# Packed compression, two VectorE jobs moved to ScalarE, and the gates last in the hybrid mixers

## The chip, the core and the metric

The kernel runs on one core of one Trainium2 chip. The metric is the device time of one execution in microseconds (us), lower is better. TensorE multiplies; VectorE (DVE in the profile), ScalarE (ACT) and GpSimd (POOL) do the rest; SyncE (SP) issues most weight loads.

## The reference, cut to what matters

Two blocks of two layers each transform a 256 x 1024 activation in float32. Every layer is a SwiGLU feed-forward, a mixer, and a second feed-forward. The change touches only the mixer of the second block (twice per execution). That mixer projects the normalised activation to many parts and runs three kinds of attention on them: stick-breaking attention (4 heads), NSA attention (8 heads, with a compressed, a selected and a window branch) and DSA attention (4 heads, keys picked by an index). Three gates then weigh their projections:

```python
def nsa_compress(x, pe, w1, w2):      # 256 tokens -> 15 blocks of 32 tokens, stride 16, 2 groups
    blocks = blocks + pe
    flat = blocks.reshape(15, 2, 32 * 64)
    return silu(flat @ w1) @ w2       # w1: 2048 x 128, w2: 128 x 64

kc = rms_norm(nsa_compress(k_cmp, ...)); vc = nsa_compress(v_cmp, ...)
g_a, g_b, g_c = split(sigmoid(h @ w_gate), 3)
merged = g_a * (o_a @ w_br_a) + g_b * (o_b @ w_br_b) + g_c * (o_c @ w_br_c)
return merged @ w_out
```

The compression yields 30 rows (15 blocks, 2 groups) of keys and 30 of values.

## The kernel before, in words

Dense products (`dense`, line 134 to 136 inside `mm3`) split every float32 weight tile into a high and a low part: a ScalarE cast (line 330) and a VectorE subtraction (line 331), two 128 x 512 weight rows at a time, called a pair here. Each pair then takes 12 matmuls (2 weight rows, 2 token tiles, 3 products). Weights arrive as units of 1 MB through SP (line 107) into a pool `raw` of 4 slots. In `mixer2` the split parts live in three slots of high parts and as many of low parts. Dense results accumulate in the PSUM pool `acc` (3 banks), attention in `at` (4 banks).

`mixer2` (from line 684) first defines its pieces and then calls them one by one at the end. Six `chunk_*` calls are dense products that give the queries, keys and values, with norms and rotations on VectorE behind them. `nsa(kz, vo, br, t, p)` is one attention step: two to four matmuls for the scores (line 880), a softmax and the product with the values in `attend` (lines 361 to 394), and the scaled result into `ob` (line 890 for branch 1, line 892 for branch 2, which adds). `attend` transposes the probabilities P by four TensorE instructions (line 385), copies them out of PSUM on VectorE (line 387), and multiplies them with the values (line 392). `dsa` uses it too, and so does the first block's `mixer1`, which passes its mask as a list. There are 15 such steps in a `mixer2`. `index` and `topk` (16 rounds, lines 843 and 844) choose DSA's keys. `stick` is the stick-breaking attention, `cmp` the compressed branch.

`compress` (line 656) runs once for keys and once for values: it transposes a piece of `z`, adds a position term on VectorE (line 665), loads `w1` (1 MB, line 667) into a `raw` slot and runs 16 accumulating float32 matmuls with 30 weight columns and 128 moving columns (line 672). A sigmoid, a product, a transpose of 30 rows (line 677) and one matmul with `w2` (line 681) follow. A float32 matmul is two TensorE instructions, each with its own weight load, so 16 matmuls are 32 instructions.

`gate(c)` is a dense product over 8 weight rows: two loads, four pairs, 48 matmuls, and two ScalarE copies out of PSUM (line 944). There are six. The sigmoid is applied later through tanh (line 1003).

The order in which each engine gets its instructions is not the order of the text: the framework schedules while it simulates a timeline, takes the earlier instruction in program order where several are ready, and so fixes a static order per engine. Moving a call in the text moves its priority. After the last piece the three results are transposed (line 229) and multiplied with `w_br_*`, and the result with `w_out`.

Of the kernel before, what the change touches and what calls it, by code (L numbers as in the profile page):

```python
# [10 lines left out]
F32 = mybir.dt.float32  # L11
F32R = mybir.dt.float32r
I32 = mybir.dt.int32
AF = mybir.ActivationFunctionType
ALU = mybir.AluOpType
# [3 lines left out]
P = 128  # L19
# [7 lines left out]
class Net:  # L27
# [332 lines left out]
    def attend(self, sc, ns, v, mask=None):  # L360
        nc = self.nc
        w = ns * P
        nh = 4 // ns
        nm = self.sm.tile([P, nh], F32, name=self.nm("nmx"), tag=f"nmx{nh}")
        src = sc
        if mask is None:
            nc.vector.tensor_reduce(nm, sc.rearrange("p (h e) -> p h e", h=nh), axis=AX, op=ALU.max, negate=True)
        else:
            src = self.b("ms")
            for j in range(nh):  # L370
                s = slice(j * w, (j + 1) * w)
                m = mask[j] if isinstance(mask, list) else mask
                nc.vector.tensor_tensor_reduce(out=src[:, s], in0=sc[:, s], in1=m, scale=1.0, scalar=-3e38,
                                               op0=ALU.add, op1=ALU.max, accum_out=nm[:, j : j + 1])
            nc.vector.tensor_single_scalar(nm, nm, -1.0, op=ALU.mult)  # L375
        den = self.sm.tile([P, nh], F32, name=self.nm("den"), tag=f"den{nh}")
        pr = self.b("pr")
        for j in range(nh):
            s = slice(j * w, (j + 1) * w)
            nc.scalar.activation(pr[:, s], src[:, s], AF.Exp, bias=nm[:, j : j + 1], accum_out=den[:, j : j + 1])  # L380
        rc = self.sm.tile([P, nh], F32, name=self.nm("rc"), tag=f"rc{nh}")
        nc.vector.reciprocal(rc, den)
        tp = sc
        for q in range(4):
            nc.tensor.transpose(tp[:, q * P : (q + 1) * P], pr[:, q * P : (q + 1) * P], self.ident)  # L385
        pt = self.b("pt")
        nc.vector.tensor_copy(pt, tp)
        po = tp
        for j in range(nh):
            for st in range(ns):  # L390
                q = slice((ns * j + st) * P, (ns * j + st + 1) * P)
                nc.tensor.matmul(po[:, j * 64 : (j + 1) * 64], lhsT=pt[:, q], rhs=v(j, st), start=(st == 0),  # L392
                                 stop=(st == ns - 1))
        return po[:, : nh * 64].rearrange("p (j d) -> p j d", j=nh), rc
# [164 lines left out]
class Mix2:  # L559
    def consts2(self):  # L560
        nc, a = self.nc, self.a
        self.c2r = self.cst2.tile([P, 4, P], F32R, name="c2r")
        st = self.raw.tile([P, 4, 512], F32, name="rawc2", tag="raw").rearrange("p a b -> p (a b)")[:, :512]
        nc.scalar.dma_start(out=st, in_=a["c2m"])
        nc.scalar.copy(self.c2r.rearrange("p a b -> p (a b)"), st)
        self.mcaus, self.mstr, self.ntri, self.none = (self.c2r[:, i] for i in range(4))
        self.idr = self.cst2.tile([P, P], F32R, name="idr")
        nc.scalar.copy(self.idr, self.ident)
        self.mc32 = self.cst2.tile([P, 2 * P], F32, name="mc32")
        nc.gpsimd.memset(self.mc32[:, :P], 0.0)  # L570
        nc.scalar.dma_start(out=self.mc32[:, P:], in_=a["c2m"][:, 0:P])
        self.c2v = self.cst2.tile([P, 288], F32, name="c2v")
        nc.scalar.dma_start(out=self.c2v[:, :286], in_=a["c2v"])
        v = self.c2v
        tt = lambda q: q.rearrange("p (t d) -> p t d", t=2)
        self.rope = (tt(v[:, 0:32]), tt(v[:, 32:48]), tt(v[:, 48:64]))
        self.ropei = (tt(v[:, 64:80]), tt(v[:, 80:88]), tt(v[:, 88:96]))
        self.cmpm = tt(v[:, 96:126])
        self.ropec = (v[0:30, 126:142].unsqueeze(1), v[0:30, 142:150].unsqueeze(1), v[0:30, 150:158].unsqueeze(1))
        self.expand = v[0:30, 158:278]  # L580
        self.bmask = v[0:120, 278:286]
        self.one = self.cst2.tile([P, 32], F32, name="one")[:, :1]
        nc.gpsimd.memset(self.one, 1.0)
        self.pet = self.cst2.tile([P, 2, 2, 16], F32, name="pet")
        nc.scalar.dma_start(out=self.pet, in_=a["pet"])

# [66 lines left out]
        self.nc.scalar.copy(kz[0:64, 0, :], tp[0:64, :256])  # L653
        self.nc.vector.tensor_copy(kz[64:128, 1, :], tp[64:128, :256])

    def compress(self, l, kv, z, hid):
        nc, a = self.nc, self.a
        tp = self.tpair(lambda g, t: z[:, t, (kv * 2 + g) * P : (kv * 2 + g + 1) * P])
        xg = self.b("rl")[:, :480].rearrange("p (k g c) -> p k g c", k=16, g=2)
        for lp in range(2):  # L660
            b = slice(64 * lp, 64 * lp + 64)
            tv = tp[b].rearrange("p (g c k) -> p k g c", g=2, k=16)
            pe = lambda k0: self.pet[b, l, kv, k0 : k0 + 8].unsqueeze(2).unsqueeze(2).broadcast_to([64, 8, 2, 15])
            for hf in range(2):
                nc.vector.tensor_tensor(xg[b, hf * 8 : hf * 8 + 8], tv[:, lp::2, :, hf : hf + 15], pe(hf * 8), op=ALU.add)
        w1 = self.raw.tile([P, 4, 512], F32, name=self.nm("w1"), tag="raw").rearrange("p a (b n) -> p (a b) n", n=P)
        nc.sync.dma_start(out=w1, in_=a["nsa_cmp_w1_2"][l, kv].rearrange("(k p) n -> p k n", p=P))
        w2 = self.b("cw2", 64)
        nc.scalar.dma_start(out=w2, in_=a["nsa_cmp_w2_2"][l, kv])
        ph = self.psum(self.at)  # L670
        for k in range(16):
            nc.tensor.matmul(ph[:30, :P], lhsT=xg[:, k].rearrange("p g c -> p (g c)"), rhs=w1[:, k],  # L672
                             start=(k == 0), stop=(k == 15))
        th = self.b("cth", P, pp=30)
        self.sigm(th, ph[:30, :P])
        nc.vector.tensor_mul(th, th, ph[:30, :P])
        nc.tensor.transpose(ph[:, P : P + 30], th, self.ident[:30, :30])
        hT = self.b("chT", 32)[:, :30]
        nc.vector.tensor_copy(hT, ph[:, P : P + 30])
        po = ph[:30, 256:320]  # L680
        nc.tensor.matmul(po, lhsT=hT, rhs=w2, start=True, stop=True)
        nc.vector.tensor_copy(hid, po)

    def mixer2(self, l, nxt):
        nc, a = self.nc, self.a
# [78 lines left out]
            return z  # L764

        def compress(z):
            self.compress(l, 0, z, hk)
            self.compress(l, 1, z, vc)
            hv = hk.unsqueeze(1).unsqueeze(1)
            self.headnorm(hv, 1, 1, [(0, 1, gn(1))], 0, pp=30)  # L770
            self.do_rope(hv, self.ropec, 8, 1, 1, pp=30)
            dup = self.b("dup", P, 1, pp=30)
            vec.tensor_copy(dup.rearrange("p (a d) -> p a d", a=2), hk.unsqueeze(1).broadcast_to([30, 2, 64]))
            tp = self.psum(self.at)
            nc.tensor.transpose(tp[:, :30], dup, self.ident[:30, :30])
            vec.tensor_copy(kcz[0:64, 0, :], tp[0:64, 0:15])
            vec.tensor_copy(kcz[64:128, 1, :], tp[64:128, 15:30])
            pv = tp
            mm(pv[:120, :64], lhsT=self.expand, rhs=vc, start=True, stop=True)
            vx = self.b("vx", 64, 1, pp=120)  # L780
            vec.tensor_copy(vx, pv[:120, :64])
            vec.tensor_tensor(vbd, vx.unsqueeze(1).broadcast_to([120, 8, 64]),
                              self.bmask.unsqueeze(2).broadcast_to([120, 8, 64]), op=ALU.mult)
# [90 lines left out]
        def nsa(kz, vo, br, t, p):  # L874
# [10 lines left out]
            for i in range(nu):  # L885
                for j in range(2):
                    o = ob[:, t, (4 * j + p + i) * 64 : (4 * j + p + i + 1) * 64]
                    k = 2 * i + j
                    if br == 1:
                        vec.tensor_scalar(out=o, in0=po[:, k], scalar1=rc[:, k : k + 1], scalar2=None, op0=ALU.mult)  # L890
                    else:
                        vec.scalar_tensor_tensor(o, po[:, k], rc[:, k : k + 1], o, op0=ALU.mult, op1=ALU.add)

# [57 lines left out]
        nsa(kzs, 256, 1, 0, 0)  # L951
        nsa(kzs, 256, 1, 1, 1)
        nsa(kzs, 256, 1, 1, 2)
        gate(0)
        chunk_b()
        nsa(kzs, 256, 1, 0, 2)
        chunk_d()
        w0 = index(0)
        nsa(kzs, 256, 1, 1, 3)
        w1 = index(1)  # L960
        nsa(kzw, 384, 2, 0, 2)
        nsa(kzw, 384, 2, 1, 3)
        chunk_f()
# [1 line left out]
        topk(1, w1)  # L965
        stick(0)
        nsa(kzw, 384, 2, 0, 0)
        gate(1)
        compress(zc)
        nsa(kzw, 384, 2, 1, 0)  # L970
        nsa(kzw, 384, 2, 1, 1)
        gate(4)
        stick(1)
        cmp(0)
        nsa(kzw, 384, 2, 1, 2)
        cmp(1)
        gate(2)
        gate(3)
        dsa(0, 0)
        dsa(1, 0)  # L980
        gate(5)
        dsa(1, 1)

        oT = {}
        for nm_, o, kk in (("a", oa, 2), ("b", ob, 4), ("c", oc, 2)):
# [171 lines left out]
```

## Time and profile before

| | us |
|---|---|
| median of 3 runs (2275.8 to 2280.51) | 2279.7 |
| the profiled execution's own time | 2279.99 |
| its span, first to last instruction | 2278.2 |
| TensorE busy in the span | 2255.0 |
| VectorE, ScalarE, GpSimd busy | 1548.1, 1148.5, 78.1 |

Times in the rows are counted from the span's start. TensorE's instructions are pipelined: an instruction's own duration holds the way through the array, and the next one starts before it ends. What an instruction costs TensorE is therefore the distance from its start to the next start. PE is the matmul side, PEld the weight loads beside it; an arrow in brackets names what ended an engine's idle time.

### The profile page before, as it was taken

What the parts mean: (1) busy time and instruction counts of PE and PEld (TensorE: products, weight loads), DVE (VectorE), ACT (ScalarE), POOL (GpSimd) and SP (SyncE); (2) the same over time, 40 slices, a digit from 0 to 9 for tenths busy, and PEclk for the clock granted to TensorE, in tenths of its full rate; (3) what the DMA queues carried; (4) which work ended last, traced back from release to release, by engine and by line L of the source; (5) the groups of instructions that cost most, each with busy time, mean ns of one, the idle gap of its engine ahead of it and who ended that gap; (6) DMA issues with size and microseconds to landing.
All of it is one profiled execution on the core that took longest, in us unless ns stands there. A gap on an engine that the chain in (4) does not pass through costs nothing.

```text
span 2278.2 us, 27621 instructions
## 1 busy us (share of the span) xinstructions
PE 2255.0 (99%) x10446; PEld 1858.3 (82%) x10446; DVE 1548.1 (68%) x2549; ACT 1148.5 (50%) x1674; POOL 78.1 (3%) x133
## 2 busy tenths in 40 slices
PE   9999999999999999999999999999999999999999
PEld 7888888888788888887888887788887888778787
DVE  5667766665666776667576896766656678877564
ACT  5445545454454545445454555554544455465443
POOL 0001000000001000000000000000000000000000
PEclk9999999999999999999999999999999999999999
DMA  7767545766676655676776534467667755425673
GB/s 260 249 237 237 188 166 185 252 238 204 221 259 218 206 176 184 223 263 201 240 244 208 184 111 130 148 212 244 238 202 238 242 183 159 134 89 186 222 252 126
DMA packets 241669, 464.68 MB, mean 204 GB/s; under 512 B 22176, under 2 KB 47392, under 8 KB 239488
## 3 DMA queue, kind: packets, MB, share of 16 engines
q1 hardware_dynamic: 212272, 397.44, 52.6%
q0 software_dynamic: 14320, 60.69, 7.5%
q10 hardware_dynamic: 14944, 4.79, 1.1%
q8 instruction: 82, 1.34, 0.2%
q14 instruction: 51, 0.42, 0.1%
HBM read 433.00 MB, written 29.88 MB: 203 GB/s over the span
## 4 chain that ended last, share of the span: by engine, by line
PE 88%; issue 7%; DMA 3%; DVE 1%; ACT 1%; DVEq 0%; POOLq 0%; ACTq 0%
PE ps L134 27%; PE ps L135 27%; PE ps L136 27%; PE ps L392 2%; DMA hT<-hop 1%; DMA hop<-hB 1%; PE ps L385 1%; PE ps L880 1%; PE ps L672 1%; PE ps L209 1%; DVE wlo L331 0%; PE ps L825 0%; PE ps L229 0%; ACT whi L330 0%; DVE hlo L331 0%
## 5 line engine op out<-in xcount | busy, mean ns | idle before, releaser
L331 DVE TENSOR_TENSOR wlo<-raw,whi 128x1024 fp32r<-128x1024 f32 (+2 forms) x754 | 907.7, 1211 | 533.6 <-ACT whi L330 515.7
L330 ACT CAST whi<-raw 128x1024 fp32r<-128x1024 f32 (+2 forms) x754 | 777.6, 1043 | 772.7 <-PE ps L136 731.8
L135 PE MATMUL ps<-wlo,xhi 128*128 128x512 f32 (+2 forms) x2048 | 798.2, 391 | 4.3 <-DVE wlo L331 4.2
L134 PE MATMUL ps<-whi,xhi 128*128 128x512 f32 (+2 forms) x2048 | 784.4, 392 | 6.3 <-ACT whi L330 6.0
L136 PE MATMUL ps<-whi,xlo 128*128 128x512 f32 (+2 forms) x2048 | 788.2, 389 | 0.0
L135 PEld LDWEIGHTS ps<-wlo,xhi 128*128 128x128 f32 x2048 | 385.7, 188 | 85.7 <-DVE wlo L331 7.8
L134 PEld LDWEIGHTS ps<-whi,xhi 128*128 128x128 f32 x2048 | 384.1, 188 | 87.0 <-ACT whi L330 8.5
L136 PEld LDWEIGHTS ps<-whi,xlo 128*128 128x128 f32 x2048 | 385.4, 188 | 77.5 <-issue 0.5
L135 PE MATMUL ps<-wlo,hhi 128*128 128x512 f32 x704 | 273.9, 389 | 0.0
L136 PE MATMUL ps<-whi,hlo 128*128 128x512 f32 x704 | 273.9, 389 | 0.0
L134 PE MATMUL ps<-whi,hhi 128*128 128x512 f32 x704 | 271.3, 389 | 0.0
L136 PEld LDWEIGHTS ps<-whi,hlo 128*128 128x128 f32 x704 | 132.1, 188 | 27.5
L134 PEld LDWEIGHTS ps<-whi,hhi 128*128 128x128 f32 x704 | 132.2, 188 | 27.4
L135 PEld LDWEIGHTS ps<-wlo,hhi 128*128 128x128 f32 x704 | 132.1, 188 | 27.4
L84 DVE STREAM_TRANSPOSE hB<-h 128x1024 f32<-128x1024 f32 (+2 forms) x72 | 98.9, 1387 | 2.9 <-DMA hop<-hB 2.7
L331 DVE TENSOR_TENSOR hlo<-hT,hhi 128x512 fp32r<-128x512 f32 (+1 forms) x96 | 57.1, 642 | 55.5 <-ACT hhi L330 55.2
L330 ACT CAST hhi<-hT 128x512 fp32r<-128x512 f32 (+1 forms) x96 | 49.8, 582 | 85.2 <-DMA hT<-hop 85.2
L261 ACT ACTIVATE sl<-ps,rstd 128x512 f32<-128x512 f32 (+1 forms) x96 | 62.3, 651 | 50.9 <-PE ps L136 46.8
L86 POOL DMA_DIRECT2D hop<-hB x43 | 23.5, 547 | 1743.3 <-ACT whi L330 858.0
L380 ACT ACTIVATE pr<-ms,nmx 128x256 f32<-128x256 f32 (+1 forms) x112 | 51.3, 461 | 43.3 <-DVE nmx L375 38.6
L263 DVE SCALAR_TENSOR_TENSOR h<-ps,rstd,sl 128x512 f32<-128x512 f32 (+1 forms) x96 | 65.1, 698 | 3.7 <-ACT sl L261 1.9
L87 POOL DMA_DIRECT2D hT<-hop x39 | 29.5, 757 | 187.4 <-DMA hop<-hB 94.1
(352 smaller groups left out, 1708.0 us busy)
## 6 DMA issues: line engine op xcount, KB each, us to landing
raw<-in_ffn_w_gu_dram SPq DMA_DIRECT2D x80, 1024.0 KB, 5.2
raw<-in_ffn_w_in_dram SPq DMA_DIRECT2D x79, 1024.0 KB, 5.2
raw<-in_ffn_w_out_dram SPq DMA_DIRECT2D x40, 1024.0 KB, 5.5
raw<-in_ffn_w_down_dram SPq DMA_DIRECT2D x40, 1024.0 KB, 5.3
raw<-in_mix_w_in_dram SPq DMA_DIRECT2D x32, 1024.0 KB, 6.3
raw<-in_w_gate_dram SPq DMA_DIRECT2D x24, 1024.0 KB, 5.2
hop<-hB POOLq DMA_DIRECT2D x16, 1024.0 KB, 5.8
hT<-hop POOLq DMA_DIRECT2D x16, 1024.0 KB, 6.3
```

The source lines that it names most:

```text
L84: nc.vector.transpose(ov[:, :, :, t, :], src(t)[:, : nk * P].rearrange("p (k i c) -> p k c i", c=4, i=32))
L86: nc.gpsimd.dma_start(out=hop.rearrange("q (i c) n -> (q i) (c n)", c=4), in_=hb)
L87: nc.gpsimd.dma_start(out=tile[:, :n].rearrange("p (q n) -> p q n", q=4), in_=hop.rearrange("q p n -> p q n"))
L134: mm(ps[:, :n], lhsT=lh, rhs=hi, start=start, stop=False)
L135: mm(ps[:, :n], lhsT=lh, rhs=lo, start=False, stop=False)
L136: mm(ps[:, :n], lhsT=ll, rhs=hi, start=False, stop=stop)
L261: nc.scalar.activation(sl[:, :w], gs[t][:, :w], AF.Silu, scale=rs[:, t : t + 1])
L263: nc.vector.scalar_tensor_tensor(h[t][:, o : o + w], us[t][:, :w], rs[:, t : t + 1], sl[:, :w], op0=ALU.mult, op1=ALU.mult)
L330: self.nc.scalar.copy(hi, src)
L331: return self.nc.vector.tensor_sub(lo, src, hi.bitcast(F32))
L380: nc.scalar.activation(pr[:, s], src[:, s], AF.Exp, bias=nm[:, j : j + 1], accum_out=den[:, j : j + 1])
L392: nc.tensor.matmul(po[:, j * 64 : (j + 1) * 64], lhsT=pt[:, q], rhs=v(j, st), start=(st == 0), stop=(st == ns - 1))
```

## The change

The two compressions of a mixer become one call. Both inputs are prepared with 32 columns (two are zeroed by GpSimd), both `w1` are loaded, and the 32 matmuls write to four groups of 32 PSUM partitions, chosen by keys or values and by the parity of k. A product with a constant `fold` matrix adds the two parities; sigmoid, product and transpose then run once for both. The call moves ahead of the window branch. In the second mixers, P is copied out of PSUM by ScalarE, and branch 1's results are scaled by ScalarE. The six gates are called after everything else, in the order 0, 1, 4, 2, 3, 5.

```diff
@@ attend
-        nc.vector.tensor_copy(pt, tp)
+        (nc.vector.tensor_copy if isinstance(mask, list) else nc.scalar.copy)(pt, tp)
@@ consts2
+        self.fold = self.cst2.tile([P, 64], F32, name="fold")
+        nc.vector.tensor_add(self.fold, self.ident[:, :64], self.ident[:, 64:])
@@ compress
-    def compress(self, l, kv, z, hid):
+    def compress(self, l, z, hids):
+        xgs, w1s, w2s = [], [], []
+        for kv in range(2):
...
+            xg = self.b("rl").rearrange("p (k c) -> p k c", k=16)
+            nc.gpsimd.memset(xg[:, :, 30:32], 0.0)
...
+            nc.sync.dma_start(out=w1, in_=a["nsa_cmp_w1_2"][l, kv].rearrange("(k p) n -> p k n", p=P))
...
         ph = self.psum(self.at)
         for k in range(16):
-            nc.tensor.matmul(ph[:30, :P], lhsT=xg[:, k].rearrange("p g c -> p (g c)"), rhs=w1[:, k],
-                             start=(k == 0), stop=(k == 15))
-        th = self.b("cth", P, pp=30)
-        self.sigm(th, ph[:30, :P])
-        nc.vector.tensor_mul(th, th, ph[:30, :P])
-        nc.tensor.transpose(ph[:, P : P + 30], th, self.ident[:30, :30])
...
+            for kv in range(2):
+                r = 32 * (2 * (k % 2) + kv)
+                nc.tensor.matmul(ph[r : r + 32, :P], lhsT=xgs[kv][:, k], rhs=w1s[kv][:, k],
+                                 start=(k < 2), stop=(k > 13))
+        part = self.b("cpp", P, 1)
+        nc.vector.tensor_copy(part, ph[:, :P])
+        hs = ph[:64, P : 2 * P]
+        nc.tensor.matmul(hs, lhsT=self.fold, rhs=part, start=True, stop=True)
+        th = self.b("cth", P, 1, pp=64)
+        self.sigm(th, hs)
+        nc.vector.tensor_mul(th, th, hs)
+        nc.tensor.transpose(ph[:, 256:320], th, self.ident[:64, :64])
+        hT = self.b("chT", 64, 1)
+        nc.vector.tensor_copy(hT, ph[:, 256:320])
+        for kv in range(2):
+            po = ph[:30, 320 + 64 * kv : 384 + 64 * kv]
+            nc.tensor.matmul(po, lhsT=hT[:, 32 * kv : 32 * kv + 30], rhs=w2s[kv], start=True, stop=True)
+            nc.vector.tensor_copy(hids[kv], po)
@@ nsa
                     if br == 1:
-                        vec.tensor_scalar(out=o, in0=po[:, k], scalar1=rc[:, k : k + 1], scalar2=None, op0=ALU.mult)
+                        act.activation(o, po[:, k], AF.Copy, scale=rc[:, k : k + 1])
@@ order of the calls
         nsa(kzs, 256, 1, 1, 2)
-        gate(0)
         chunk_b()
...
         w1 = index(1)
+        compress(zc)
         nsa(kzw, 384, 2, 0, 2)
...
         nsa(kzw, 384, 2, 0, 0)
-        gate(1)
-        compress(zc)
         nsa(kzw, 384, 2, 1, 0)
         nsa(kzw, 384, 2, 1, 1)
-        gate(4)
         stick(1)
         cmp(0)
         nsa(kzw, 384, 2, 1, 2)
         cmp(1)
-        gate(2)
-        gate(3)
         dsa(0, 0)
         dsa(1, 0)
-        gate(5)
         dsa(1, 1)
+        for c in (0, 1, 4, 2, 3, 5):
+            gate(c)
```

## Rows read from the trace of the kernel before

**Rows 1.** The page: the chain that ended last, by engine.
```profile
PE 88%; issue 7%; DMA 3%; DVE 1%; ACT 1%; DVEq 0%; POOLq 0%; ACTq 0%
```
**Rows 2.** Stretches: busy us (instructions) of PE, PEld, DVE, ACT, POOL; PE's granted clock.
```profile
1240.00:1472.00 232.00, 231.19 (x1186) 187.46 (x1185) 188.69 (x539) 129.15 (x247) 2.89 (x7) 1.00 0.44 141
...
1330.00:1350.00 20.00, 20.00 (x91) 14.40 (x89) 19.79 (x78) 12.80 (x30) 0.00 (x0) 1.00 0.33 107
1417.00:1431.50 14.50, 13.96 (x91) 10.32 (x89) 13.26 (x61) 8.29 (x28) 0.00 (x0) 1.00 0.10 36
2023.50:2039.20 15.70, 15.16 (x90) 11.62 (x89) 13.53 (x61) 8.30 (x28) 0.00 (x0) 0.89 0.11 35
2027.40:2030.80 3.40, 3.40 (x15) 2.93 (x14) 2.47 (x15) 0.30 (x1) 0.00 (x0) 0.50 0.15 57
```
**Rows 3.** Line 672 in the first second-block mixer: count, durations (ns), first and last start.
```profile
L672 PEld LDWEIGHTS ps<-w,rl x64: 104/108/108, 1365.0 to 1376.5; 128*30 128x30 f32 x64
L672 PE MATMUL ps<-w,rl x64: 272/273/295, 1365.0 to 1376.6; 128*30 128x128 f32 x64
```
**Rows 4.** Timeline of PE around line 672: start, us, instructions merged (x how many).
```profile
1371.33 1.06 PE L672 MATMUL ps<-w,rl 128*30 128x128 f32 x8
1372.32 1.10 PE L925 MATMUL ps<-va,se 128*128 128x64 f32 x8
1373.36 1.93 PE L672 MATMUL ps<-w,rl 128*30 128x128 f32 x16
1375.22 1.10 PE L392 MATMUL ps<-va,pt 128*128 128x64 f32 x8
```
**Rows 5.** Timeline of PE where lines 681 and 677 run between dense matmuls.
```profile
1381.75 0.40 PE L135 MATMUL ps<-wlo,xhi 128*128 128x512 f32 x1
1381.99 0.40 PE L136 MATMUL ps<-whi,xlo 128*128 128x512 f32 x1
1382.32 0.30 PE L681 MATMUL ps<-cw,chT 128*30 128x64 f32 x2
1382.55 0.74 PE L134 MATMUL ps<-whi,xhi 128*128 128x512 f32 x2
1383.21 0.24 PE L677 MATMUL ps<-ident,cth 30*128 30x30 f32 x1
1383.38 0.50 PE L134 MATMUL ps<-whi,xhi 128*128 128x512 f32 x1
```
**Rows 6.** Groups of the first second-block mixer: busy us, mean ns, idle before and releasers.
```profile
L331 DVE TENSOR_TENSOR wlo<-raw,whi 128x1024 fp32r<-128x1024 f32 x54 | 65.8, 1221 | 14.6 <-ACT whi L330 14.3
L330 ACT CAST whi<-raw 128x1024 fp32r<-128x1024 f32 x53 | 55.5, 1047 | 37.8 <-PE ps L136 36.6 <-ACT whi L330 0.7
...
L387 DVE COPY pt<-ps 128x512 f32<-128x512 f32 x15 | 10.1, 685 | 0.9 <-PE ps L385 0.9
...
L890 DVE TENSOR_SCALAR ob<-ps,rc 128x64 f32<-128x64 f32 x16 | 3.7, 277 | 1.1 <-PE ps L392 1.1
...
L817 ACT COPY oth<-ps 128x512 f32<-128x512 f32 x1 | 0.6, 592 | 0.0
...
L636 ACT ACTIVATE va<-ps,rstd 128x64 f32<-128x64 f32 x1 | 0.3, 315 | 0.0
```
**Rows 7.** SP's loads in the same mixer: start, us from first to last, count.
```profile
1303.82 9.49 SPq L667 DMA_DIRECT2D w<-in_nsa_cmp_w_dram  x2
1320.96 59.98 SPq L107 DMA_DIRECT2D raw<-in_w_gate_dram  x8
```
**Rows 8.** Timeline of PE where float32 transposes fall between dense matmuls.
```profile
1403.51 0.48 PE L135 MATMUL ps<-wlo,xhi 128*128 128x512 f32 x1
1403.83 0.60 PE L385 MATMUL ps<-ident,pr 128*128 128x128 f32 x4
```
**Rows 9.** Groups of topk in the same mixer, shapes merged.
```profile
L843 DVE MAX8 m<-work 128x8 f32<-128x128 f32 (+1 forms) x16 | 5.7, 355 | 0.0
L844 DVE MATCH_REPLACE8 work<-m,work 128x128 f32<-128x128 f32 (+1 forms) x16 | 5.5, 344 | 0.0
```

More of the change, by code (lines that the diff above doesn't have):

```diff
@@ L654, in zevac @@
         self.nc.vector.tensor_copy(kz[64:128, 1, :], tp[64:128, :256])
-    def compress(self, l, kv, z, hid):
+    def compress(self, l, z, hids):
         nc, a = self.nc, self.a
[L658 to L669, printed above, removed]
+        xgs, w1s, w2s = [], [], []
+        for kv in range(2):
+            tp = self.tpair(lambda g, t: z[:, t, (kv * 2 + g) * P : (kv * 2 + g + 1) * P])
+            xg = self.b("rl").rearrange("p (k c) -> p k c", k=16)
+            nc.gpsimd.memset(xg[:, :, 30:32], 0.0)
+            xv = xg[:, :, :30].rearrange("p k (g c) -> p k g c", g=2)
+            for lp in range(2):
+                b = slice(64 * lp, 64 * lp + 64)
+                tv = tp[b].rearrange("p (g c k) -> p k g c", g=2, k=16)
+                pe = lambda k0: self.pet[b, l, kv, k0 : k0 + 8].unsqueeze(2).unsqueeze(2).broadcast_to([64, 8, 2, 15])
+                for hf in range(2):
+                    nc.vector.tensor_tensor(xv[b, hf * 8 : hf * 8 + 8], tv[:, lp::2, :, hf : hf + 15], pe(hf * 8),
+                                            op=ALU.add)
+            w1 = self.raw.tile([P, 4, 512], F32, name=self.nm("w1"), tag="raw").rearrange("p a (b n) -> p (a b) n", n=P)
+            nc.sync.dma_start(out=w1, in_=a["nsa_cmp_w1_2"][l, kv].rearrange("(k p) n -> p k n", p=P))
+            w2 = self.b("cw2", 64)
+            nc.scalar.dma_start(out=w2, in_=a["nsa_cmp_w2_2"][l, kv])
+            xgs.append(xg), w1s.append(w1), w2s.append(w2)
@@ L670, in compress @@
         ph = self.psum(self.at)
         for k in range(16):
-            nc.tensor.matmul(ph[:30, :P], lhsT=xg[:, k].rearrange("p g c -> p (g c)"), rhs=w1[:, k],
-                             start=(k == 0), stop=(k == 15))
-        th = self.b("cth", P, pp=30)
-        self.sigm(th, ph[:30, :P])
-        nc.vector.tensor_mul(th, th, ph[:30, :P])
-        nc.tensor.transpose(ph[:, P : P + 30], th, self.ident[:30, :30])
-        hT = self.b("chT", 32)[:, :30]
-        nc.vector.tensor_copy(hT, ph[:, P : P + 30])
@@ L680, in compress @@
-        po = ph[:30, 256:320]
-        nc.tensor.matmul(po, lhsT=hT, rhs=w2, start=True, stop=True)
-        nc.vector.tensor_copy(hid, po)
+            for kv in range(2):
[6 more added lines that the diff above has]
+        nc.tensor.matmul(hs, lhsT=self.fold, rhs=part, start=True, stop=True)
@@ L766, in compress @@
         def compress(z):
-            self.compress(l, 0, z, hk)
-            self.compress(l, 1, z, vc)
+            self.compress(l, z, (hk, vc))
             hv = hk.unsqueeze(1).unsqueeze(1)
```

## The prediction

> **What bounds the kernel now.** I read the chain that ended last first: it runs through TensorE for 88% of the span [rows 1]. So a microsecond counts only if it comes off TensorE's own stream, or if it opens or closes a gap in that stream. The busy time by stretch shows the second-block mixer, 232 us long, with TensorE busy for 231.19 of them, VectorE for 188.69 and ScalarE for 129.15 [rows 2]; the second layer's mixer repeats it. Even in a stretch where VectorE is busy for 19.79 of 20 us TensorE has no gap [rows 2]. The only gaps stand at the end of the attention, some 0.54 us in each layer (13.96 of 14.50, 15.16 of 15.70) [rows 2]. In the second layer that same end takes 15.70 us instead of 14.50, and 3.4 us of it have a granted clock of 0.50, the 1.2 GHz level, just after a thin stretch of short matmuls [rows 2]. So the argument goes by distances from start to start on TensorE, not by the durations in its rows.
>
> **What the compression costs TensorE now.** Per mixer line 672 issues 64 instructions [rows 3]. A run of 16 of them lasts 1.86 us until the next line starts and a run of 8 lasts 0.99 us [rows 4]; the difference, 0.87 us for 8, gives 0.109 us for each instruction, and 0.12 us remain for leaving the 30-column form. So 64 x 0.109 = 7.0 us. The other forms cannot start under this one: a dense matmul that is followed by line 681 takes 0.33 us to the next start where its neighbour takes 0.24, so entering costs 0.09; the two dense ones after it take 0.66 instead of 0.48, which is one return and the next entry, 0.09 each [rows 5]. Line 681 itself takes 0.23 and line 677 0.17 [rows 5]. In the timeline the 64 instructions, first at 1365.0 and last at 1376.6 [rows 3], come in eight runs with attention matmuls between them: 8 x (0.12 + 0.09) = 1.7 us. The two visits of line 681 cost 0.41 each, those of line 677 0.35 each, together 1.5. Sum: 10.2 us per mixer.
>
> **What it costs after.** There are still 32 float32 matmuls and so 64 instructions, now in four groups of 32 output partitions. The two halves of one matmul go to the same group and must follow each other; the next matmul's first half goes to another group. If groups run side by side, a pair of halves should cost one distance, not two: 32 x 0.109 = 3.5 us. No row of the profile shows two column groups, so I bound it: 7.0 us if nothing overlaps, 1.75 if all four groups do, and above 7.0 if a change of group costs what a change of form costs (below). I take 3.5, since the order of the halves forbids four at a time and since the weights of 30 columns are already hidden now (a load of 108 ns beside a matmul every 109 [rows 3, 4]). To it come: three runs rather than eight, as one accumulation holds both (3 x 0.21 = 0.6; between 1 and 8 runs 0.2 to 1.7); the fold product, two halves and a change of form, 2 x 0.109 + 0.21 = 0.4; one transpose, 0.35; the two products with w2 together, 0.41 + 2 x 0.054 = 0.5. Sum 5.4, so 4.8 us less per mixer and **9.6 us in both**.
>
> **What moves beside it.** P's copy takes 685 ns on VectorE, 15 times; ScalarE's copy of the same shape out of PSUM takes 592 [rows 6]. Branch 1's scaling takes 277 ns, 16 times, against 315 for ScalarE's scaled copy of 128 x 64 [rows 6]. VectorE goes from 189 to 174 us of the 232, ScalarE from 129 to 143. I cost this at nothing, because TensorE covers it; without that cover each attention step would be 0.1 us shorter by the copy and some 0.1 longer by the scalings. Queued behind a copy that waits for its transposes are ScalarE's weight casts, and behind those VectorE's subtractions and TensorE. What hides a late cast are the three pair slots: two further pairs are 24 matmuls, 5.8 us at 0.24 [rows 5], less 1.05 for the cast and 1.22 for the subtraction [rows 6], so a pair may be 3.5 us late. The compression's small VectorE work (one copy and one sigmoid instead of two sigmoids), the zeroing on GpSimd, busy for 2.89 of 232 us [rows 2], and the one-time fold matrix lie under the same cover.
>
> **The gates.** Moved, per mixer, are 6 x 48 = 288 dense matmuls on TensorE, 24 casts on ScalarE and as many subtractions on VectorE, 12 copies out of PSUM on ScalarE, and 12 loads on SP, past all chunks, the attention and both w1 loads; POOL's queue has nothing of them. None is added or dropped. As the lowest in order they fill what attention leaves, up to its very end. That may close the 0.54 us gaps and keep the clock at 2.4 GHz at the second layer's end: 2 x 0.54 + 1.2 = 2.3 us at best [rows 2]. Against it, float32 work between dense matmuls costs an entry each time: a dense matmul before four transposes takes 0.32 instead of 0.24 [rows 5, 8]. The end stretches hold 88 to 91 instructions in some 24 pieces each; dense work between half of them is 2 x 12 x 0.08 = 1.9 us. I put the two together at nothing, with 2 us either way. The w1 loads now claim two of the four raw slots early; they already did, from 1303.82 until line 672 ran at 1365, while gate loads went through the other two without a gap on TensorE [rows 2, 3, 7]. After the change they should be freed sooner, so I cost it at nothing.
>
> **The sum.** The profiled execution took 2279.99 us (span 2278.2 and 1.8 around it); 2279.99 - 9.6 = 2270.4. The median of the runs shown, 2279.7, lies 0.3 below, so I say **2270**.
>
> **Rivals.** **No overlap of groups (0.22).** Each instruction keeps 0.109 us. Then 7.0 + 1.9 = 8.9 instead of 10.2, 2.6 us less in all, 2277.4. This is also the case in which the packing does not do what it says; for it speaks that no row shows overlap between instructions of this form.
> **Four groups at once (0.15).** 1.75 + 1.9 = 3.7, so 6.5 less per mixer: 2267.0. Against it: halves of one group stand next to each other. The Trainium skill (TensorEngine Tiling (Array Packing), Theoretical Speedup) gives up to 4x for 32 columns; by that rule the time is this rival's, and no row here shows it.
> **A change of group drains the array (0.05).** Then every pair costs what leaving costs now, 2 x 0.109 + 0.12 = 0.34, and 32 of them 10.8 us; with the 1.9 that is 2.5 more per mixer, 2285. The start of a load beside each running matmul [rows 3, 4] speaks against it, but all these loads go to one group. The Trainium skill (TensorE: Matmul & The Clock Gate, Part 3, The mechanism) says that weight loads slip under a running matmul only where the row group differs. All four column groups use the same 128 rows, so by it the change would go this rival's way; rows 3 and 4 disagree, as load and matmul of the same rows fit in one distance.
> **The gates starve (0.14), slower.** Their casts and subtractions are last in order on both engines. If VectorE runs topk's dependent rounds, 5.7 + 5.5 = 11.2 us per mixer [rows 9], in one block ahead of a waiting subtraction, the 3.5 us of cover run out and TensorE stands for 7.7 us: per mixer 2.9 more than now, 2285.8. It decides from 4.8 us of gap per mixer on. For it: gate 0 stood ahead of topk in order, and VectorE is busy for 19.79 of 20 us there [rows 2]. Against it: the change takes 14 us off VectorE, and chunks go first.
>
> **How the numbers follow.** The forecast has 0.44. A measurement of this kernel tells about 0.2% from no change, 4.6 us. Forecast and four groups are faster: 0.59. No overlap is within: 0.22. Drain and starving are slower: 0.19. The range reaches from four groups with the better clock (2267.0 - 2.3, about 2264) to no overlap with the bad end, many runs and a part of a starved gate (2282); it leaves out the 0.19 that are slower.
>
> **What would show it.** Right: line 672's successor still 64 instructions per mixer, with pairs 0.11 us apart, few runs, TensorE busy throughout, the last dense matmuls of a gate after the last attention matmul, and no 0.50 clock at the second mixer's end. Wrong: distances of 0.109 throughout (no overlap), 0.03 (four groups) or 0.17 on average (drain); gaps on TensorE ended by lines 330 or 331 (starving), or ScalarE casts that wait behind P's copy.

## The result, and the profile after

The changed kernel is slower: 2311.27 us median of 6 runs (2303.52 to 2316.35) against 2280.11 of 6 before (2275.8 to 2282.56), ratio 1.0136 [1.0117, 1.0155]. The forecast was 2270 with a range to 2282. The profiled execution took 2310.99, 31.0 more than the one of before.

Lines of after differ by some ten to fifteen: the compression's matmuls are line 682, its fold product 687, its transpose 691, the product with `w2` 696, the transpose of `dup` (the compressed keys written twice, for the score product) 789, an NSA step's scores 894, stick's scores 913, a gate's copy out of PSUM 958, tanh 1013; 920 to 922 are stick's functions on ScalarE, 874 the exponential of `cmp`. Four lines of the page (span, PE's busy time, the PE clock in 40 slices, the chain that ended last):

```profile
span 2309.2 us, 27640 instructions
...
PE 2268.2 (98%) x10448; PEld 1864.8 (81%) x10448; DVE 1527.7 (66%) x2482; ACT 1180.6 (51%) x1742; POOL 78.8 (3%) x137
...
PEclk9999999999999999999999997999999999989999
...
PE 83%; issue 7%; DMA 4%; DVE 3%; ACT 2%; DVEq 0%; ACTq 0%; POOLq 0%
```

TensorE's share of the chain fell from 88% [rows 1] to 83%, and two slices have a lower clock, one in each second-block mixer. The view of stretches gives the place (PE, PEld, DVE, ACT, POOL busy; PE's granted clock):

```profile
1392.00:1460.00 68.00, 58.03 (x269) 45.06 (x268) 35.68 (x122) 41.43 (x85) 0.00 (x0) 0.81 0.20 62
2015.00:2082.00 67.00, 57.26 (x270) 44.66 (x269) 36.02 (x122) 41.81 (x85) 0.00 (x0) 0.82 0.19 63
1400.00:1420.00 20.00, 15.65 (x74) 11.86 (x74) 10.23 (x45) 14.16 (x32) 0.00 (x0) 0.74 0.09 29
1420.00:1440.00 20.00, 17.02 (x58) 12.16 (x56) 9.71 (x46) 7.24 (x21) 0.00 (x0) 0.66 0.00 1
```

The ends of the attention, 0.54 us of idle TensorE each before [rows 2], now hold 9.97 and 9.74 us of it, and the mean clock there is 0.81 and 0.82, a mix of the 2.4 and the 1.2 GHz level. At those clocks 68 and 67 us lose 0.19 x 68 + 0.18 x 67 = 25.0 us' worth of work, against 1.7 before (3.40 us at 0.50 [rows 2]). By this estimate the ends cost 18.6 + 23.3 us; less the 13.0 that the packing should bring with four groups side by side, that is 28.9 of the 31.0. It is no more than an estimate, since some of the low clock falls on idle time and so is counted twice. It puts the loss at the two ends, gap and clock at about the same weight; the lengths of the two mixers, read below, are 30.4 us more together.

Why the ends are bare shows in TensorE's timeline of the first such mixer (start, us, instructions merged; the dense ones left out):

```profile
1342.03 1.00 PE L392 MATMUL ps<-va,pt 128*128 128x64 f32 x8
1342.96 0.41 PE L682 MATMUL ps<-w,rl 128*32 128x128 f32 x2
...
1350.74 1.95 PE L682 MATMUL ps<-w,rl 128*32 128x128 f32 x62
...
1357.81 0.43 PE L687 MATMUL ps<-cpp,fold 128*64 128x128 f32 x2
...
1365.74 0.27 PE L691 MATMUL ps<-ident,cth 64*128 64x64 f32 x1
1370.26 0.30 PE L696 MATMUL ps<-cw,chT 128*30 128x64 f32 x2
1374.85 0.30 PE L696 MATMUL ps<-cw,chT 128*30 128x64 f32 x2
1383.50 0.24 PE L789 MATMUL ps<-ident,dup 30*128 30x30 f32 x1
1383.67 1.99 PE L894 MATMUL ps<-nsaT 128*128 128x256 f32 x6
1385.50 1.02 PE L913 MATMUL ps<-oth 128*128 128x512 f32 x2
```

Two things stand here. The 62 instructions start over 1.87 us, 0.030 each instead of 0.109: four groups do run side by side. And from 1343 to 1383.5 no step of the attention starts, though the inputs of the window branch are there (the one-bank kernel below starts it), and those of stick from 1360 on, when its last copy (line 831) has run; the window branch (894) and stick (913) start 0.17 and 2.0 us after `dup`. It is not that the banks of `at` run out: the result of the last step before is read out by 1343.6, and until `dup` only the compression's lines write to that pool (the transposes of line 646, left out here, use another), so three of the four banks stand unused. What holds the steps up is the order in which banks are handed out. TensorE filled those 40 us with the last chunk and with gates. What was left to cover the rest is in the view of two lines over 1240 to 1480 (first and last start):

```profile
L958 ACT ACTIVATE th<-ps,rh x10: 687/690/704, 1321.4 to 1381.1; 128x512 f32<-128x512 f32 x10
L958 ACT ACTIVATE zc<-ps,rh x2: 669/670/670, 1397.0 to 1399.9; 128x512 f32<-128x512 f32 x2
...
L392 PE MATMUL ps<-va,pt x120: 217/275/454, 1307.6 to 1453.8; 128*128 128x64 f32 x120
```

The last gate is out at 1399.9 and the last attention product starts at 1453.8: an **uncovered end** of 54 us, in which short matmuls wait for softmax steps. It was 18 before, where the same view has 1415.3 and 1433.7:

```profile
L944 ACT ACTIVATE zc<-ps,rh x2: 688/690/692, 1414.7 to 1415.3; 128x512 f32<-128x512 f32 x2
...
L392 PE MATMUL ps<-va,pt x120: 217/275/323, 1305.3 to 1433.7; 128*128 128x64 f32 x120
```

The chain in this end shows one more cost (start, us, what):

```profile
1397.73 1.28 ACT L922
...
1401.49 1.28 ACT L1013
...
1418.34 1.28 ACT L922
...
1420.59 1.09 ACT L874
```

These are ScalarE's table loads, 1.28 us each (of the last, 1.09 lie on the chain): gates done early bring their tanh (1013) between stick's logarithm (922) and the exponentials, and the table is exchanged each time: seven loads per mixer against three before.

### The profile page after: what moved, and what is told of

Its sections match the earlier page's. It is cut to its first block, busy times and chain, and to the rows that moved or that the text cites. A ratio compares the mean times of both kernels' runs of the same rounds, so it can differ in the third digit from the quotient of the medians.

```text
span 2309.2 us, 27640 instructions
## 1 busy us (share of the span) xinstructions
PE 2268.2 (98%) x10448; PEld 1864.8 (81%) x10448; DVE 1527.7 (66%) x2482; ACT 1180.6 (51%) x1742; POOL 78.8 (3%) x137
## 4 chain that ended last, share of the span: by engine, by line
PE 83%; issue 7%; DMA 4%; DVE 3%; ACT 2%; DVEq 0%; ACTq 0%; POOLq 0%
PE ps L134 26%; PE ps L135 26%; PE ps L136 25%; DMA hT<-hop 2%; DMA hop<-hB 2%; PE ps L392 2%; DVE wlo L331 1%; PE ps L385 1%; PE ps L894 1%; DVE hlo L331 1%; ACT whi L330 1%; PE ps L209 1%; PE ps L839 0%; PE ps L229 0%; PE ps L646 0%
## 5 line engine op out<-in xcount | busy, mean ns | idle before, releaser
L385 PE MATMUL ps<-ident,pr 128*128 128x128 f32 x184 | 34.7, 296 | 2.3 <-ACT pr L380 2.3
```

## The experiments

**Theory 1.** The pool `at` has four banks and hands them out in program order. The compression takes two (its own, and one for `dup` and the product with `expand` at the end of its chain), so what stands behind it in the text gets no bank until that chain is nearly through, even while other banks are free. Gates use the pool `acc`, run alone, and are used up. **Rival 2:** the gates' last place makes the bare end. **Rival 3:** the ScalarE moves do.

Two distances are read from each profile. The mixer's length goes from the table load that opens a second-block mixer to the start of the last product of tanh and branch (lines 1004 and 1014); it leaves out how the rest of an execution drifts. The uncovered end goes from the start of the last gate copy to the start of the last product with the values (line 392), in the first layer. The profiled execution was the shortest of its kernel's runs in e3, e7 and e8 and the longest in e1b and e11; the lengths of e3, whose four runs lie far apart, are low by it. "Early" and "late" is the compression's place, ahead of the window branch or as before.

| kernel | compression | gates | on ScalarE | ratio to before | both lengths against 423.1 | uncovered end |
|---|---|---|---|---|---|---|
| before | late, 3 banks | spread | no | | | 18.3 |
| after | early, packed, 2 banks | last | yes | 1.0136 [1.0117, 1.0155] | +30.4 | 54.0 |
| e1b_one_bank | early, packed, 1 | last | yes | 0.9935 [0.9910, 0.9959] | -13.5 | 14.5 |
| e13_one_bank_gates_back | early, packed, 1 | spread | yes | 0.9950 [0.9925, 0.9974] | -13.2 | 14.5 |
| e8_packed_one_bank | late, packed, 1 | spread | no | 0.9979 [0.9966, 0.9992] | -10.3 | 14.8 |
| e11_back_one_bank | late, packed, 1 | last | yes | 0.9999 [0.9975, 1.0024] | -7.1 | 17.4 |
| e7_gates_last_only | late, 3 banks | last | no | 1.0010 [0.9998, 1.0022] | -0.5 | 18.3 |
| e9_one_bank_dve | early, packed, 1 | last | no | 1.0005 [0.9981, 1.0029] | +1.0 | 24.1 |
| e6_act_only | late, 3 banks | spread | yes | 1.0007 [0.9993, 1.0022] | +2.1 | 17.9 |
| e5_packed_only | late, packed, 2 | spread | no | 1.0057 [1.0042, 1.0072] | +7.7 | 32.4 |
| e2_compress_back | late, packed, 2 | last | yes | 1.0051 [1.0038, 1.0065] | +12.9 | 33.0 |
| e10_early_only | early, 3 banks | spread | no | 1.0101 [1.0082, 1.0120] | +15.6 | 35.6 |
| e3_gates_back | early, packed, 2 | spread | yes | 1.0123 [1.0072, 1.0175] | +17.1 | 48.9 |

**One bank.** `dup` and `expand` go to 64 free columns of the compression's own bank; nothing else differs from the kernel after.

```diff
+        return ph[:, 448:512]
...
-            self.compress(l, z, (hk, vc))
+            tp = self.compress(l, z, (hk, vc))
...
-            tp = self.psum(self.at)
```

> The kernel after with one change: the transpose of dup and the product with expand use free columns of the compression's own PSUM bank, so the compression holds one bank of the pool of four instead of two. Calls, packing and ScalarE moves stay as in the kernel after. Theory 1 (the attention steps behind the early compression cannot get a PSUM bank until the last link of the compression's chain has its own, and the gates are used up meanwhile): attention matmuls start again between 1343 and 1383 us, the stretch at the end without dense matmuls shrinks, and the 31 us come back together with the cheaper compression, 2266 to 2282. Rival 2 (the gates' last place alone makes the uncovered end): no bank changes that, 2300 to 2312. Rival 3 (P's copy and the scaling on ScalarE lengthen every attention step): 2305 to 2312.

Measured 2271.15 (2266.24 to 2275.45). Theory 1 holds, both rivals fall as causes of the whole. Its timeline and stretches:

```profile
1350.88 1.89 PE L894 MATMUL ps<-nsaT 128*128 128x256 f32 x6
...
1371.53 1.02 PE L913 MATMUL ps<-oth 128*128 128x512 f32 x2
...
1393.11 0.24 PE L789 MATMUL ps<-ident,dup 30*128 30x30 f32 x1
```
```profile
1400.00:1420.00 20.00, 20.00 (x109) 16.55 (x108) 11.27 (x29) 15.18 (x26) 0.00 (x0) 1.00 0.32 104
1420.00:1440.00 20.00, 19.29 (x114) 15.03 (x114) 13.70 (x51) 13.19 (x36) 0.00 (x0) 1.00 0.09 27
```

The window branch and stick now run 42 and 22 us ahead of `dup`, TensorE is busy and the clock is 1.00. `dup` itself is no earlier within the mixer (138.9 us after the opening table load, against 136.5 in the kernel after): not the chain got shorter, but what waited for it.

**The compression back at its old place** (the call moved behind `nsa(kzw, 384, 2, 0, 0)`).

> The kernel after with the call of the compression back behind the first step of the window branch that stood ahead of it before; the gates stay last, packing and ScalarE moves stay. Theory 1 (place of the compression): 2264 to 2280, since stick and the window branch no longer queue for a bank behind it. Rival 2 (gates last): as the kernel after, 2300 to 2312. Rival 3 (ScalarE moves): 2305 to 2312.

Measured 2296.08, over Theory 1's range. Somewhat more than half of the loss comes back (ratio 1.0051 for 1.0136), not all; so the place is not the whole cause.

**The gates back, and the gates alone.** First the kernel after with each `gate(c)` at its old place, then the kernel before with the loop `for c in (0, 1, 4, 2, 3, 5): gate(c)` at the end.

> The kernel after with the six gates back at their old places between the attention steps; the compression stays ahead of the window branch. Theory 1: the attention still waits for the compression's bank and ScalarE's and TensorE's cover still runs out, 2305 to 2316. Rival 2 (gates last): the late gates cover the end again, 2266 to 2282. Rival 3: 2305 to 2312.

> The kernel before with only the six gates moved behind the last attention step; unpacked compression at its old place, no ScalarE moves. Theory 1: no change, 2276 to 2284, since the attention starts as early as before. Rival 2 (gates last): slower by most of the 31 us, 2298 to 2312. Rival 3: 2276 to 2284.

Measured 2310.59 and 2284.93, the second 0.9 us over Theory 1's range, with an interval of the ratio that holds 1. The gates' place explains nothing: without the early compression it costs nothing that can be told, with it nothing that can be told is won by undoing it. Rival 2 falls.

**The parts alone.** Packing alone; the ScalarE moves alone; the unpacked compression early and nothing else; packing alone in one bank.

> The kernel before with the packed compression alone: old order of all calls, P's copy and the first branch's scaling on VectorE. Theory 1 (the attention behind the compression waits for its second bank; whatever shortens TensorE's work ahead of that moment without making the moment earlier only uses the gates up sooner): the matmul work of the compression falls by some 7 us a mixer, but less dense gate work is left behind the dup transpose, so the end of the attention is uncovered: 2282 to 2298. The prediction on record, which took the packing alone for 9.6 us: 2266 to 2274. Rival 3 (ScalarE moves are the cost): 2266 to 2276.

> The kernel before with P's copy and the first branch's scaling on ScalarE alone; unpacked compression, old order. Theory 1: no change worth telling, 2276 to 2285. Rival 3 (the longer ScalarE steps lengthen the attention's chain): 2288 or more.

> The kernel before with the call of the unpacked compression moved ahead of the window branch and nothing else. Theory 1: the window branch and stick queue for a PSUM bank behind the compression's last link here too, and the end runs uncovered: 2292 to 2315. If the early place only hurts together with the packing or with the late gates: 2276 to 2285.

> The packed-only kernel with dup's transpose and the product with expand in free columns of the compression's own bank; old order, no ScalarE moves. Theory 1: attention steps go on during the compression's chain, dense gate work is left for the end, and the packing's gain shows: 2264 to 2276. If the bank matters only at the early place: as the packed-only kernel.

Measured 2295.64, 2284.38, 2306.04 and 2278.2. The last missed its range (2264 to 2276) by 2.2 us; the others are in Theory 1's. Rival 3 falls with e6. The early call alone gives 24 of the 31 us; its timeline has the picture of the kernel after:

```profile
1379.15 0.24 PE L775 MATMUL ps<-ident,dup 30*128 30x30 f32 x1
1379.32 1.99 PE L880 MATMUL ps<-nsaT 128*128 128x256 f32 x6
1381.15 1.02 PE L899 MATMUL ps<-oth 128*128 128x512 f32 x2
```

That packing alone is slower is the finding that the prediction had no place for. Its timeline and a stretch:

```profile
1409.86 0.24 PE L789 MATMUL ps<-ident,dup 30*128 30x30 f32 x1
1410.03 1.98 PE L894 MATMUL ps<-nsaT 128*128 128x512 f32 x4
1411.85 1.02 PE L913 MATMUL ps<-oth 128*128 128x512 f32 x2
```
```profile
1420.00:1440.00 20.00, 19.32 (x76) 14.12 (x76) 13.64 (x63) 9.83 (x25) 0.00 (x0) 0.66 0.08 26
```

`dup` comes 153.7 us after the opening table load, where before it came at 147.7: one chain for keys and values, with a fold more, ends later than the keys' own chain did, although its matmuls are shorter. The kernel before waited for that bank too. The matmuls taken off TensorE had covered part of this wait; gates took their place, and the last gate is out 6.7 us after `dup` instead of 20.8: 6.0 of these 14.1 us because `dup` is later, 8.1 because the gates are through sooner. How the two share the loss, no run separates. With the bank taken away (e8) the same packing wins 0.2%, and the lengths 18.0 us against e5.

**The rest of the one-bank kernel.** Without the ScalarE moves; at the old place; with the gates at their old places.

> The one-bank kernel (early packed compression, gates last) with P's copy and the first branch's scaling back on VectorE. Theory 1, with the ScalarE moves worth nothing by themselves: within 0.3% of the one-bank kernel's 2271, 2264 to 2278. If the ScalarE moves are what makes the early place pay (VectorE free for topk and the split): 2278 to 2292.

> The kernel with the compression back at its old place, gates last, packing and ScalarE moves, and now dup and expand in the compression's own bank. Theory 1 (the bank is the cause at the old place too, where the two-bank form took 2296): 2264 to 2278. If the old place is slow for a reason of its own: 2288 to 2300.

> The one-bank kernel with the six gates back at their old places. Theory 1 with the gates' place worth nothing while the attention is not held up: 2266 to 2278. If the gates' last place is needed for the cover once the bank is free: 2280 to 2295.

Measured 2287.04, 2283.38 and 2271.34. The gates again change nothing. The ScalarE moves, nothing by themselves (e6), are worth 14.5 us of the lengths in the one-bank kernel (e1b against e9, which missed Theory 1's range and fell in the other). In e9 the fifteen copies of P in a mixer start on average 0.87 and 1.10 us (first and second layer) after the end of their last transpose, among topk's rounds and the subtractions on VectorE; in e1b 0.36 and 0.40. That topk's rounds are what holds the steps up is argued from these times; no run took them away. At the late place the moves win nothing: e11 has them and e8 has not (they differ in the gates' place too), and e11 is no faster. Nor is the early place good by itself: without the moves, in one bank, its lengths are 11.3 us longer than at the late place (e9 against e8). e11 missed its range (2264 to 2278): 12.7 us better than its two-bank form, but not fast.

Three pairs differ in the bank alone, and in each the one-bank kernel is faster: after and e1b by 43.9 us of the lengths, e2 and e11 by 20.0, e5 and e8 by 18.0. So the second bank costs time at either place, with the other changes and without.

**The price of the four groups.** The order of the 32 products, in the one-bank kernel: two groups in turn in the first layer, one after the other in the second.

```diff
-        for k in range(16):
-            for kv in range(2):
-                r = 32 * (2 * (k % 2) + kv)
+        for i in range(32):
+            k, kv, h = (i // 2, i % 2, i // 16) if l == 0 else (i % 16, i // 16, (i // 8) % 2)
+            r = 32 * (2 * h + kv)
...
-                                 start=(k < 2), stop=(k > 13))
+                             start=(k % 8 == 0), stop=(k % 8 == 7))
```

> The one-bank kernel with another order of the 32 compression products: in the first layer two column groups in turn, 16 products in each pair of groups; in the second layer one group at a time, eight products in a row. Same products, same sums. Read from the timeline of the line. If the four groups of the kernel after really run side by side (0.030 us an instruction): two in turn about 0.055 to 0.06, one at a time about 0.109 as in the kernel before, so the 64 instructions last some 1.9, 3.6 and 7.0 us. If the short distance came from the smaller tile alone and not from the overlap: 0.03 in all three. The whole: within 0.4% of the one-bank kernel.

The timeline of the line, first layer, then second:

```profile
1352.93 3.28 PE L682 MATMUL ps<-w,rl 128*32 128x128 f32 x62
...
1951.38 3.06 PE L682 MATMUL ps<-w,rl 128*32 128x128 f32 x30
1960.01 3.27 PE L682 MATMUL ps<-w,rl 128*32 128x128 f32 x32
```

62 instructions last 3.28 us with two groups, 1.95 with four (above); one group at a time takes 3.27 for 32, twice as long as two. In the single starts a step is 0.109 us: one instruction starts in it with one group, two with two groups, four with four, some 7 ns apart. The mixer lasts 204.8 us with four groups (e1b, both layers 204.7 to 204.9), 206.0 with two and 209.9 with one, so the overlap is worth 5.1 us a mixer, 1.3 of them an uncovered end that is longer with one group. So the short distance is overlap, not the smaller tile. The whole took 2279.38 in one run.

## Why the prediction was wrong

- **What bounds the kernel** (TensorE's stream, gaps at the attention's end): right as a reading. But "the only gaps stand at the end" was taken as a fact about the work, and it was one about the order: just enough gates were left to cover it. The table's two last columns go together: the kernels with an end of 14.5 to 14.8 us are the fastest, those above 30 us the slow ones.
- **The compression's price.** "32 x 0.109 = 3.5" was mis-sized; rival "four groups" was right with 1.75 (measured 1.9). The reason given, that the order of the halves forbids four at a time, does not hold: sets of four start 7 ns apart. Which halves stand in such a set, no row tells. The runs of line 682 were two instead of three, and the products with `w2` came in two visits, not together. By rival four groups' terms the mixers would be 13.0 us shorter; the one-bank kernel's are 13.5 shorter, but that match is in part luck, since its uncovered ends are also 3.9 and 5.1 us shorter. What the overlap alone is worth is e12's 5.1 us a mixer. The Trainium skill (TensorEngine Tiling (Array Packing), Theoretical Speedup) gave up to 4x for 32 columns, and e12 agrees with it: four starts to a step with four groups, one with one. The Trainium skill's other rule that was weighed (TensorE: Matmul & The Clock Gate, Part 3, The mechanism), loads hidden only where the row group differs, is not borne out here: all four groups use the same 128 rows, and their loads are hidden at four per 0.109 us. The same section also lets a load go ahead into a background weight buffer, which no row here can tell.
- **"I cost it at nothing"**, said of the ScalarE moves: right by themselves (e6), but they pay at the early place once the attention no longer waits for a bank (e1b against e9). Nothing was said of that.
- **The gates, "I put the two together at nothing":** right (e7; e13 against e1b).
- **The step that failed** is the last of the parts: "After the change they should be freed sooner, so I cost it at nothing". Of the compression's move ahead of the window branch it counted the w1 loads' slots and none of the queues that the call is moved past. PSUM's pool `at` is one, handed out in program order, with the compression's second bank asked for at the end of a chain of 40.5 us (line 682's first start at 1342.96 to `dup` at 1383.50). The move alone cost 24 us (e10), and without the second bank the kernel after is 43.9 us of the lengths faster (e1b). The kernel's code shows who draws from the pool (the scores of line 880, stick, lines 672 and `dup`), and the profile of before already had the wait, with its next step of the window branch 0.17 us after `dup`:

```profile
1394.54 0.24 PE L775 MATMUL ps<-ident,dup 30*128 30x30 f32 x1
1394.71 1.98 PE L880 MATMUL ps<-nsaT 128*128 128x512 f32 x4
```

- **The second failed step** is the sum itself: it took every microsecond off TensorE as gained, and put the small steps between the matmuls "under the same cover". In e5 the matmuls saved had been cover for a wait, the chain of those small steps ended 6.0 us later, and 0.57% was lost.
- **The rivals.** "The gates starve" ended on the right side for another reason: no gate waited for topk; they ran too soon.
- **What would show it wrong:** distances of 0.03 came as stated for four groups. Gaps ended by lines 330 or 331 were to show starving; the chain at the end shows ScalarE's table loads and softmax steps instead.

What stays open: how much of e9's loss is VectorE's queue, and whether e11 really gains less than e8, since the intervals of their ratios overlap.

## What to carry to other kernels

When a call is moved, list every pool that its pieces draw from and ask who gets the next buffer, and when; a buffer that is asked for at the end of a long chain holds up all that stands behind it, even work whose data is ready. Give such a chain's last small results room in a buffer that it already has: a change of three lines turned +1.4% into -0.65%. And independent filler work is a stock: before taking work off the bounding engine, look at what that work covers and whether the filler still reaches to the end.

## What the runs showed of the hardware

Float32 matmuls with 32 weight columns in four column groups start four to a step of 0.109 us, weight loads and all, and with one, two or four groups in turn one, two or four start in a step (e12). A ScalarE table exchange takes 1.28 us, and in the kernel after, where tanh comes between logarithm and exponential, four of the seven loads in a mixer lie on the chain. In a stretch of short matmuls with gaps (1420 to 1440 of the kernel after) the granted clock fell to a mean of 0.66 over 20 us, though TensorE counted as busy for 17.02 of them: there, busy time alone hides the loss.
